# Rotary tables read back on GpSimd's queue, pooling-weight products in a fresh pair of tiles, value weights behind the query rows

## The chip, the cores and the metric

The kernel runs on one core of one Trainium2 chip. The metric is the device time of one execution in microseconds. The kernel before took 2415.74 us (median of 3 runs, 2414.28 to 2416.57).

A core has five engines with a queue each, worked off in order: PE (TensorE, matrix products into PSUM), ACT (ScalarE), DVE (VectorE), POOL (GpSimd) and SP (SyncE). An instruction that waits for a semaphore holds up everything behind it on its engine. Transfers are issued from the queues of SP, ACT and POOL; the instruction that issues one waits in its queue like any other, until the data to be sent are there and the place to be filled is free.

## The reference

One layer of a decoder trunk in float32, for 2048 tokens of width 1024 and 256 memory tokens:

```python
h = rmsnorm(x, mix_norm_g)
q, k, v, g, u = split(h @ w_in)                   # 4 heads of 128; u: 4 groups of 128 channels
y_ret  = silu(g) * head_rmsnorm(retention(rope(q), rope(k), v))
y_pool = pool_mixer(u, pool_w, pool_scale)        # trailing means, then a 128x128 product per group
x = x + concat(y_ret, y_pool) @ w_out
x = x + cross_attn(rmsnorm(x), rmsnorm(mem), wq, wkv, wo)
x = x + conv_glu_ffn(rmsnorm(x), w_up, conv, w_down)
return rmsnorm(x, final_norm_g)
```

`rope` turns each pair of halves of a head by an angle `position * inv_freq`: `t1 cos - t2 sin`, `t2 cos + t1 sin`.

## The kernel before

**Precision.** Every large product is made of three passes of TensorE: an operand is split into a rounded part (ACT, line 259 or 262) and a remainder (DVE, line 243 or 251), and high x high, high x low and low x high are added in PSUM (lines 271 to 273). So each weight tile costs, before it can be used, a load, two activations of 512 columns and two vector operations.

**Tiles and places.** SBUF is handed out in slots. `raws` are five places of 4 KB per partition for loaded weights, used in turn; `prs` are places for split pairs, to which free slots of the arenas G and E are lent; `Z` has eight slots of 4 KB per partition, `TT` (shown as T) ten of half that. A slot that is taken again waits for whatever still reads or writes it, a transfer from it included. `take()` hands out the slot that has been free for longest.

**Folded weights.** Two products of weights are made once, so that later stages need fewer: `folded_weights` is a generator of 32 steps that the program runs in portions, `folded(n)`. Steps 1 to 16 project the memory to keys and values (the values go to DRAM, `Vd`). Steps 17 to 20 (one per head) multiply the keys with the query weights: two loads of rows of `wqT` by `row_pairs` (line 497), 48 products of 256 columns, and the result to DRAM (`Md`, lines 548 and 501). Step 21 loads the pooling weights and three rows of `wout_p`; steps 22 to 24 multiply the four pooling groups `g` with their rows of the output projection (evacuation L592) and send each to DRAM (`WPd`, L594), and load `Vd` (L606). Steps 25 to 32 multiply the memory's values with `wo` (evacuation L633, stores to `VWd` L634).

In the loop over `g`, groups 0 and 1 take a Z slot each, and groups 2 and 3 write into the same two slots again.

**Opening.** Steps 1 to 20 run while tokens are loaded (`xR` for the norm, `xT` for the operand X), one step per turn `n` of a loop. In turns 16 to 19 the program calls `value_weights(n - 16)` (two rows of `w_v` into a raw place, split into a slot of G for the first two and of E for the others) and then `folded(1)`, which is one head of the query weights. After the loop come `values` (192 products), and beside them in `between()` the sums of quarters of X (`quarter_sums`) and, from the third call on, one step of `rope_steps(0)` per call.

**Rotary tables.** `rope_steps` loads the positions (two small transfers), computes sine and cosine on DVE in 11 steps in six T slots, and stores three tiles (sine, cosine, minus sine) to `rope_d`, on SP's queue (L2005). `scaled_tables`, a step generator inside the head projections, takes two Z slots, reads them back in four transfers on SP's queue (L1611), goes on with four steps of other splits, and then multiplies both tables with the norm's factors (four vector operations). They are used first where the second of eight pairs of projections is finished (`final`, kind < 2). Each of 56 items of the head projections (12 products of 512 columns) calls `step()` twice.

**Head projections to output projection.** The last items of the heads call steps 21, 22 and 23; after them come `folded(2)`, one more step for each step that is left of the last head's retention, and the output projection's eight `unit`s. Unit n loads four blocks of `wout_r` (L2118) and four of `WPd` (L2119) into one raw place and makes 48 products; block 4, the first one of `WPd`, is the fourth of the order. After units 0, 1 and 2 come 1, 2 and 4 more calls of `folded`.

**Sums of weights.** `weight_sums` adds blocks of the MLP's weights in DRAM by accumulating transfers from POOL's queue. It moves on by one round for every `spacing[0]` calls of `next(under[0])`, which `units` makes twice per unit if `paced[0]` is set. Before, it begins in the attention after the output projection of the first 1024 tokens.

**Order.** The order of instructions on each engine is set by a planner that runs over the program with its own estimate of times: earlier program order goes first where several are ready. `keep_in_program_order` and `issue_after` fix single places.

## Time and profile before

| | |
|---|---|
| runs, us | 2414.28, 2416.57, 2415.74 |
| profiled execution, us | 2421.08 |
| its span, us | 2419.3 |
| PE busy, us | 2390.1 (99%) |
| DVE, ACT, POOL busy, us | 1734.0 (72%), 1350.3 (56%), 276.0 (11%) |
| mean granted clock of TensorE | 0.997 |
| moved by DMA, MB | 511.53 |

A busy time is the union of an engine's instructions. A matmul of 512 columns is recorded as 0.38 us and starts 0.23 us after the one before it, so a PE that never waits shows 20.00 us of 20 and some 90 matmuls of that size. The chain of work that ended last is on PE for 94% of the span. The time that PE does not work is 29.2 us in all, and the views by windows tell in which stretches it lies.

### The profile page before, as it was taken

What the parts mean: (1) busy time and instruction counts of PE and PEld (TensorE: products, weight loads), DVE (VectorE), ACT (ScalarE), POOL (GpSimd) and SP (SyncE); (2) the same over time, 40 slices, a digit from 0 to 9 for tenths busy, and PEclk for the clock granted to TensorE, in tenths of its full rate; (3) what the DMA queues carried; (4) which work ended last, traced back from release to release, by engine and by line L of the source; (5) the groups of instructions that cost most, each with busy time, mean ns of one, the idle gap of its engine ahead of it and who ended that gap; (6) DMA issues with size and microseconds to landing.
All of it is one profiled execution on the core that took longest, in us unless ns stands there. A gap on an engine that the chain in (4) does not pass through costs nothing.

```text
span 2419.3 us, 33286 instructions
## 1 busy us (share of the span) xinstructions
PE 2390.1 (99%) x11186; PEld 1993.0 (82%) x11186; DVE 1734.0 (72%) x2904; ACT 1350.3 (56%) x2488; POOL 276.0 (11%) x437
## 2 busy tenths in 40 slices
PE   9999999999999999999999999999999999999998
PEld 8888878888888888888888888888888888887886
DVE  7787774754667665665789776987677698877876
ACT  7654564443445543434555555755555577676673
POOL 0010000063034444100001000110000000000000
PEclk9999999999999999999999999999999999999999
DMA  9732187499688799785477554765455479757952
GB/s 360 262 122 90 63 269 231 135 255 329 194 231 218 188 244 322 195 283 191 140 243 258 184 190 131 251 194 183 158 175 185 134 257 314 238 178 265 345 180 74
DMA packets 267451, 511.53 MB, mean 211 GB/s; under 512 B 29184, under 2 KB 58384, under 8 KB 267280
## 3 DMA queue, kind: packets, MB, share of 16 engines
q1 hardware_dynamic: 209312, 402.30, 50.1%
q0 software_dynamic: 32768, 77.61, 13.1%
q10 hardware_dynamic: 25200, 29.49, 3.5%
q8 instruction: 88, 1.44, 0.2%
q14 instruction: 83, 0.68, 0.1%
HBM read 397.61 MB, written 180.89 MB: 239 GB/s over the span
## 4 chain that ended last, share of the span: by engine, by line
PE 94%; DMA 2%; ACT 2%; DVE 1%; issue 0%; SPq 0%; ACTq 0%; DVEq 0%
PE mm L271 29%; PE mm L272 29%; PE mm L273 29%; PE aux L271 1%; PE aux L273 1%; PE aux L272 1%; ACT G L259 1%; PE aux L901 1%; DMA WPd<-Z 1%; PE aux L778 1%; DVE Z L243 1%; PE aux L806 1%; PE aux L790 0%; PE aux L808 0%; DMA R<-wkv 0%
## 5 line engine op out<-in xcount | busy, mean ns | idle before, releaser
L271 PE MATMUL mm<-G,Q 128*128 128x512 f32 (+1 forms) x1631 | 624.7, 384 | 6.9 <-ACT Q L259 2.7
L273 PE MATMUL mm<-G,Q 128*128 128x512 f32 (+1 forms) x1631 | 619.8, 383 | 0.8 <-DVE Q L243 0.8
L272 PE MATMUL mm<-G,Q 128*128 128x512 f32 (+1 forms) x1503 | 574.1, 382 | 0.2 <-DVE G L251 0.2
L272 PE MATMUL mm<-G,E 128*128 128x512 f32 (+1 forms) x1092 | 420.7, 385 | 0.0
L271 PE MATMUL mm<-G,E 128*128 128x512 f32 (+1 forms) x1092 | 419.2, 386 | 0.5 <-ACT E L259 0.5
L273 PE MATMUL mm<-G,E 128*128 128x512 f32 (+1 forms) x1092 | 418.4, 385 | 0.4 <-DVE E L243 0.4
L271 PEld LDWEIGHTS mm<-G,Q 128*128 128x128 f32 x1631 | 307.0, 188 | 69.2 <-ACT Q L259 4.0
L273 PEld LDWEIGHTS mm<-G,Q 128*128 128x128 f32 x1631 | 306.8, 188 | 60.6 <-DVE Q L243 1.8
L272 PEld LDWEIGHTS mm<-G,Q 128*128 128x128 f32 x1503 | 283.0, 188 | 53.5 <-DVE G L251 0.4
L243 DVE TENSOR_TENSOR Z<-Z,mm 128x512 f32<-128x512 f32 (+1 forms) x322 | 216.4, 676 | 124.6 <-PE mm L273 121.8
L251 DVE SCALAR_TENSOR_TENSOR Z<-Z,vecs 128x1024 f32<-128x1024 f32 x176 | 224.9, 1282 | 50.3 <-ACT Z L1134 48.0
L271 PEld LDWEIGHTS mm<-G,E 128*128 128x128 f32 x1092 | 205.3, 188 | 41.8 <-ACT E L259 0.7
L273 PEld LDWEIGHTS mm<-G,E 128*128 128x128 f32 x1092 | 205.3, 188 | 41.8 <-DVE E L243 0.7
L272 PEld LDWEIGHTS mm<-G,E 128*128 128x128 f32 x1092 | 205.3, 188 | 41.0
L1071 ACT ACTIVATE E<-R 128x512 fp32r<-128x512 f32 (+1 forms) x165 | 101.6, 616 | 146.9 <-PE mm L272 138.7
L243 DVE TENSOR_TENSOR Q<-R,Q 128x512 fp32r<-128x512 f32 x174 | 119.0, 688 | 53.0 <-ACT Q L259 34.7
L243 DVE TENSOR_TENSOR T<-T 128x512 f32<-128x512 f32 (+4 forms) x189 | 130.0, 692 | 23.4 <-ACT T L432 12.0
L243 DVE TENSOR_TENSOR G<-T,G 128x512 fp32r<-128x512 f32 (+1 forms) x173 | 113.8, 678 | 32.4 <-ACT G L1018 18.9
L1018 ACT ACTIVATE G<-T 128x512 fp32r<-128x512 f32 x186 | 111.8, 623 | 36.5 <-DMA T<-Gd 28.6
L1134 ACT ACTIVATE Z<-Z,vecs 128x1024 f32<-128x1024 f32 x88 | 109.2, 1242 | 31.8 <-DVE Z L243 30.8
L1071 ACT ACTIVATE E<-S 128x512 fp32r<-128x512 f32 (+1 forms) x107 | 65.9, 616 | 108.8 <-PE mm L272 106.9
L243 DVE TENSOR_TENSOR E<-R,E 128x512 fp32r<-128x512 f32 (+1 forms) x133 | 89.3, 675 | 43.8 <-ACT E L1071 43.1
(348 smaller groups left out, 3948.3 us busy)
## 6 DMA issues: line engine op xcount, KB each, us to landing
T<-Gd SPq DMA_DIRECT2D x173, 256.0 KB, 4.3
Ud<-w_up POOLq DMA_DIRECT2D x132, 256.0 KB, 9.1
Gd<-Z SPq DMA_DIRECT2D x110, 256.0 KB, 2.6
R<-Ud SPq DMA_DIRECT2D x106, 256.0 KB, 2.8
R<-w_up SPq DMA_DIRECT2D x80, 256.0 KB, 3.1
S<-Ud SPq DMA_DIRECT2D x70, 256.0 KB, 2.9
Gd<-T SPq DMA_DIRECT2D x56, 256.0 KB, 3.3
S<-w_up SPq DMA_DIRECT2D x52, 256.0 KB, 3.1
```

What stands on the lines that cost most here:

```text
L243: return eng.tensor_tensor(out=out, in0=a, in1=b, op=op)
L251: return dve.scalar_tensor_tensor(out=out, in0=a, scalar=s, in1=b, op0=op0, op1=op1)
L259: one = act.activation(hi, src, AF.Copy)
L271: pe.matmul(ps, lh, rh, start=start, stop=False, skip_group_check=more)
L272: pe.matmul(ps, lh, rl, start=False, stop=False, skip_group_check=more)
L273: latest[0] = pe.matmul(ps, ll, rh, start=False, stop=stop, skip_group_check=more)
L778: pe.matmul(col(sc, c), self.ch(k, c), self.ch(q, c), start=True, stop=True)
L806: pe.matmul(col(y, c), col(self.pr.f, c), self.ch(v, c, h * T), start=True, stop=self.cur[c] is None)
L901: pe.transpose(tp[:, j * P : (j + 1) * P], e.f[:, j * P : (j + 1) * P], ident)
L1018: one = act.activation(hi, x, AF.Copy, scale=-1.0 if i == 2 else 1.0)
L1071: act.activation(p2[:, 0, :w], self.raw[i].f[:, :w], AF.Copy)
L1134: act.activation(self.c[g].f, a[:, 2:], AF.Identity, bias=cb[:, f : f + 1], scale=cw[2][:, f : f + 1])
```

## The change

Five edits, all before or within the first half of the tokens:

1. Pooling groups 0 and 1 take, write and free a Z slot each; groups 2 and 3 share a fresh pair of neighbouring slots and go to DRAM in one transfer of 1 MB (three transfers for four).
2. The two halves (`mt`) of a step of the `wo` products are laid side by side and stored in one transfer instead of two.
3. The rotary tables of the first 1024 tokens: `rope_steps(0)` is begun, with five steps, at the end of the opening loop, and goes on by a step at every call of `between()`; its three stores are issued on ACT's queue, its four reads on POOL's; four empty steps are put ahead of the scaling.
4. `value_weights(0)` comes behind the second head's step of the query weights, 1 behind the third, 2 and 3 behind the fourth; the step goes first in each turn.
5. Calls of `folded` around the output projection: 2 instead of 1 per step of the last retention, then 2, 2, 2 after the units instead of 1, 2, 4. `paced` is set after the third unit, with a spacing of 3, instead of after the eighth.

```diff
-        vp4, held = G[:, 8 * T : 12 * T].rearrange("p (n i m) -> p n i m", i=2, m=NMEM), []
-        ended = []
+        vp4, ended = G[:, 8 * T : 12 * T].rearrange("p (n i m) -> p n i m", i=2, m=NMEM), []
         for g in range(4):
             u = ahead.pop(0)
-            if g < 2:
-                held.append(Z.take())
-            t = held[g % 2]
+            if g < 3:
+                held = Z.take(1 + g // 2)
+                t = held.f.rearrange("p (n k c) -> p n k c", n=KT, c=P)
...
-                done = act.activation(t.f[:, nh * SUB : (nh + 1) * SUB], ps, AF.Copy)
+                done = act.activation(t[:, 4 * nh : 4 * nh + 4, g % (held.n)], ps.rearrange("p (n c) -> p n c", c=P), AF.Copy)
             ended.append(done)
-            act.dma_start(WPd[:, :, g, :].rearrange("n p c -> p n c"), t.f.rearrange("p (n c) -> p n c", n=KT))
-            if g > 1:
-                t.free()
+            if g != 2:
+                act.dma_start(WPd[:, :, g + 1 - held.n : g + 1, :].rearrange("n p k c -> p n k c"), t)
+                held.free()
...
-                out = t.f[:, mt * SUB : (mt + 1) * SUB]
-                ended.append(act.activation(out, ps, AF.Identity, scale=rn[:, mt : mt + 1]))
-                act.dma_start(tiles4(VWd, nh, 2 * h + mt), out.rearrange("p (n c) -> p n c", n=4))
+                out = t.f.rearrange("p (n k c) -> p n k c", n=4, c=P)
+                ended.append(act.activation(out[:, :, mt], ps.rearrange("p (n c) -> p n c", c=P), AF.Identity, scale=rn[:, mt : mt + 1]))
+            act.dma_start(VWd[4 * nh : 4 * nh + 4, :, 2 * h : 2 * h + 2, :].rearrange("n p k c -> p n k c"), out)
...
-                sp.dma_start(out.f[p, i * T : (i + 1) * T].rearrange("p (s c) -> p s c", s=NS), rope_d[b][to].rearrange("(s p) c -> p s c", s=NS))
+                (sp if b else pool).dma_start(out.f[p, i * T : (i + 1) * T].rearrange("p (s c) -> p s c", s=NS), rope_d[b][to].rearrange("(s p) c -> p s c", s=NS))
...
             z.free(2, 2)
+            for _ in range(0 if b else 4):
+                yield
...
-            sp.dma_start(rope_d[b][i], r.f[:, :SUB])
+            (sp if b else act).dma_start(rope_d[b][i], r.f[:, :SUB])
...
+    tables = rope_steps(0)
     for n in range(1, 2 * KT + HEADS):
...
-        if 2 * KT <= n < 2 * KT + 4:
-            wv.append(value_weights(n - 2 * KT, B.arenas[(n - 2 * KT) // 2]))
         folded(1)
+        for kp in {2 * KT + 1: (0,), 2 * KT + 2: (1,), 2 * KT + 3: (2, 3)}.get(n, ()):
+            wv.append(value_weights(kp, B.arenas[kp // 2]))
+    for _ in range(5):
+        next(tables)
     reclaim(spare)
...
-        tables = iter(()) if b else rope_steps(0)
+        tables = iter(()) if b else tables
...
-            if place[0] > 2:
-                next(tables, None)
+            next(tables, None)
...
             for _ in behind[0]:
-                folded(1)
+                folded(2)
...
-                folded((1, 2, 4, 0, 0, 0, 0, 0)[n])
-        paced[0] = True
+                folded((2, 2, 2, 0, 0, 0, 0, 0)[n])
+                if n == 2:
+                    paced[0], spacing[0] = True, 3
```

## The prediction

> **What bounds the kernel now.** I read the busy table first (PE 99%), then busy time by windows, to see where the missing 29.2 us lie:

> ```profile
> core 0: us, PE busy (x) PEld busy (x) DVE busy (x) ACT busy (x) POOL busy (x), PEclk, DMA share, GB/s
> 0.00:80.00 80.00, 71.08 (x551) 68.53 (x552) 60.17 (x124) 66.03 (x125) 0.20 (x4) 1.00 0.95 352
> 80.00:280.00 200.00, 198.96 (x1011) 168.69 (x1011) 158.77 (x306) 99.67 (x209) 17.78 (x32) 1.00 0.38 127
> 280.00:360.00 80.00, 73.87 (x349) 58.81 (x348) 62.98 (x129) 55.14 (x124) 0.00 (x0) 0.98 0.61 203
> 360.00:780.00 420.00, 420.00 (x1947) 349.01 (x1946) 248.67 (x482) 186.74 (x382) 111.76 (x173) 1.00 0.79 229
> ```

> The change can win only where PE waits: 8.9 us in the opening, 1.0 in the head projections, 6.1 around the output projection. From 360 to 780 nothing is to be had. So this is a matter of at most some 16 us of 2416, and each edit is costed by the wait that it touches.

> **Value weights behind query rows.** In the opening, PE waits twice for ACT while the query weights are multiplied (waits of PE from 60 to 90, then ACT's timeline from 62 to 76):

> ```profile
> PE mm L271 <- ACT G L259: 3.4, 2, 2.2
> ...
> 62.82 0.63 ACT L259 ACTIVATE G<-S 128x512 fp32r<-128x512 f32 x1
> 63.34 0.63 ACT L259 ACTIVATE G<-S 128x512 fp32r<-128x512 f32 x1
> 66.00 0.67 ACT L259 ACTIVATE G<-R 128x512 fp32r<-128x512 f32 x1
> 67.04 0.68 ACT L259 ACTIVATE E<-R 128x512 fp32r<-128x512 f32 x1
> 68.61 0.66 ACT L259 ACTIVATE E<-R 128x512 fp32r<-128x512 f32 x1
> 69.12 0.66 ACT L259 ACTIVATE G<-R 128x512 fp32r<-128x512 f32 x1
> ...
> 60.00:80.00 20.00, 16.57 (x133) 15.96 (x132) 14.34 (x21) 18.86 (x41) 0.00 (x0) 1.00 0.95 322
> ```

> PE resumes on the activations at 66.00 and 69.12, splits of query rows. Ahead of the first stand two splits of value weights (62.82 and 63.34), ahead of the second two more (E, 67.04 and 68.61; E only ever holds value weights 2 and 3 here). ACT is busy for 18.86 of these 20 us, so it is the bound, and what leaves its queue ahead of a query row is won: four splits at a pitch of 0.52 us (63.34 less 62.82) are 2.1 us of the 3.4. Row loads also come sooner, since value weights no longer take a raw place ahead of them, so the wait can go whole. Bounds 0 (ACT's work is the same, and stays the limit) and -3.4; I take **-2.3**, near the counted splits. What the splits wait for afterwards: `values` needs weights 2 and 3 only after 24 products, 5.3 us into it (90 products take 20 us in the row of 100 to 120 below). The next 200 us of PE are dense (198.96 of 200), so time won here isn't lost behind it unless the tables are late.

> **Rotary tables.** Waits of DVE and of SP from 100 to 150, then of PE from 140 to 312:

> ```profile
> DVE Z L243 <- DMA Z<-rope: 4.4, 2, 3.1
> ...
> SPq L2005 <- ACT T L724: 10.2, 1, 10.2
> ...
> PE mm L271 <- DVE T L243: 0.3, 1, 0.3
> ```

> DVE stood 4.4 us for the tables, and SP 10.2 us for the sine with loads behind it; of all this 0.3 us reached PE, when a sum on DVE came late (0.4 with the restart). The tables' five first steps go 10 us and more earlier, to where DVE is not full:

> ```profile
> 80.00:100.00 20.00, 20.00 (x114) 17.60 (x114) 12.37 (x21) 11.65 (x25) 0.00 (x0) 1.00 0.98 340
> 100.00:120.00 20.00, 20.00 (x90) 16.57 (x89) 19.93 (x36) 7.92 (x13) 2.38 (x4) 1.00 0.36 129
> ...
> Z<-rope SPq DMA_DIRECT2D x4, 256.0 KB, 3.8
> Ad<-R POOLq DMA_DIRECT2D x22, 256.0 KB, 2.7
> ...
> Ud<-w_up POOLq DMA_DIRECT2D x132, 256.0 KB, 9.1
> ```

> The reads on POOL cost the price of its stores of the same size in the same stretch (100 to 300), 2.7 us to landing, and queue behind at most a few of those; SP is free for the projections' loads. The three stores on ACT are issues beside 7.92 busy us of 20. Four empty steps are two items of 12 products, 5.3 us; the first use comes three items (8.0 us) after the new place. I take **-0.4**; bounds -0.4 and 0: if the reads land as late as the slowest kind on POOL's queue (9.1 us, `Ud`), they are 5.3 us later than on SP (3.8), which the empty steps just cover.

> [...]

> **Pooling weights.** The waits of PE, then of ACT, from 320 to 350, the chain of that stretch, and two rows of ACT's timeline:

> ```profile
> PE mm L271 <- ACT Q L259: 2.0, 2, 1.3
> PE mm L271 <- ACT Z L592: 0.6, 1, 0.6
> PE mm L271 <- ACT Z L633: 0.6, 1, 0.6
> PE mm L271 <- DVE T L243: 0.5, 1, 0.5
> ...
> ACT Q L259 <- DMA R<-WPd: 4.2, 1, 4.2
> ACT G L259 <- DMA S<-Vd: 2.9, 1, 2.9
> ...
> 327.90 7.24 DMA WPd<-Z
> 336.28 5.61 DMA WPd<-Z
> 341.98 5.39 DMA R<-WPd
> ...
> 330.33 1.10 ACT L592 ACTIVATE Z<-mm 128x512 f32<-128x512 f32 x2
> 335.16 0.60 ACT L592 ACTIVATE Z<-mm 128x512 f32<-128x512 f32 x1 [1.59 <-DMA WPd<-Z]
> ```

> This is the change's main place. Group 3 is evacuated at 335.16 because its Z slot is still being stored (group 1's transfer, 7.24 us). ACT stands 1.6 us, and with it the evacuations and splits behind it; PE waits 1.3 us for a split (Q L259) and 0.6 for L633. Only then can group 3 be stored (5.61 us) and read back for unit 0 (5.39), which holds ACT 4.2 us and PE 0.7 more, the second wait for Q L259. With a fresh pair, group 3 follows group 2, which ACT evacuated at 330.33, so its store can go out by 332, over 4 us sooner, and one more `wo` step (12 products, 2.7 us) stands ahead of unit 0. That removes the waits of 2.0 and 0.6 us. PE was also slowed after these waits:

> ```profile
> 340.74 0.78 PE L273 MATMUL mm<-G,Q 128*128 128x512 f32 x1
> 341.31 0.63 PE L271 MATMUL mm<-G,Q 128*128 128x512 f32 x1
> 341.74 0.56 PE L272 MATMUL mm<-G,Q 128*128 128x512 f32 x1
> 342.13 0.39 PE L273 MATMUL mm<-G,Q 128*128 128x512 f32 x1
> ...
> 320.00:340.00 20.00, 16.98 (x75) 12.41 (x75) 16.63 (x41) 15.18 (x42) 0.00 (x0) 0.97 0.86 275
> 340.00:360.00 20.00, 19.31 (x83) 15.25 (x82) 12.17 (x19) 11.12 (x22) 0.00 (x0) 0.95 1.02 356
> ```

> Starts 0.57, 0.43 and 0.39 us apart, where 0.23 is usual, under a granted clock of 0.97 and 0.95: 0.03 and 0.05 of 20 us are 1.6 us of clock, of which I count 1.5. In all 2.0 + 0.6 + 1.5 = 4.1. The waits for L592 and DVE (1.1 us) come from `Vd` (2.9 us of ACT), which stays. The bounds: -5.2 with those too; and on the bad side one megabyte where half a one went. Two half ones took 7.24 and 5.61; if the one takes both, 12.9 us, it lands at 344.9, is read by 350.3, later than 347.37 by 2.9, against the 2.7 us of the extra step: nothing is won at unit 0, but the 1.3 and 0.6 us of the held ACT are. I take **-3.6**, half a microsecond short of the count, since DVE with 16.63 and ACT with 15.18 of 20 us will be nearer to full once the waits are out.

> [...]

> **The rest at nothing.** Side-by-side stores of the `wo` products halve issues on ACT, whose pace there is set by transfers. Sums of weights begin in units 3 to 7, in the stretch from 360 to 780 (first view), where PE is busy for 420.00 of 420 us, with and without POOL's sums beside it (111.76 us). Ten calls at a spacing of 3 are four rounds; the attention then makes two fewer of its own, so that the sums are two rounds ahead of before. The cover is the load ahead: if it went, a unit would wait for a load about once. I take 0, bounds 0 and +1.

> **The sum.** -2.3 - 0.4 - 3.6 = -6.3 us. The profiled execution took 2421.08 us for a span of 2419.3, so 1.8 us lie around the span and stay; it would take 2414.8. It is 5.3 us above the median of the runs, which is not of one place, so the same -6.3 us goes on the median: **2409.4 us**.

> **Rivals.**

> A. *The opening is not paid.* ACT's order changes, but its 18.86 of 20 us stay the limit, and other work (the split of X between the two, the evacuations) stands where the value weights stood. For it: the total work is the same. Against: half of it is needed only 5.3 us later. Time: -0.4 - 3.6, 2411.7.

> B. *The pooling wait moves.* The one megabyte lands as late as both halves, and ACT is held by `Vd` and the read as before. For it: a DMA share of 0.86 and 1.02 in these windows. Against: the store starts over 4 us earlier. Time: -2.3 - 0.4, 2413.0.

> C. *Slower: the positions block the opening.* The tables begin at the end of the opening, so their first T slots are those whose `Md` store is still under way, the positions' load waits for it on SP, and DVE, in order, waits for the positions. From 60 to 92:

> ```profile
> Md<-T ACTq DMA_DIRECT2D x16, 256.0 KB, 6.3
> T<-pos SPq DMA_DIRECT2D x2, 128.0 KB, 4.1
> ```

> That is 10.4 us from a store to the first table operation. If the planner, reckoning with shorter transfers, puts it on DVE ahead of the last head's low parts, PE has half a head left (24 products of 256 columns at 0.125 us, 133 in 16.57 busy us from 60 to 80, make 3.0): a stall of 7.4 us, with 1.5 of slow clock 8.9, and the opening isn't won: 8.9 - 0.4 - 3.6 = +4.9, 2420.6. It decides once the stall with its clock is over the 4.0 us that the other terms win. Against it: earlier program order goes first, and the last head's rows are loaded ahead of the positions.

> [...]

> E. *It does nothing*: the planner's new order opens as many gaps as it closes, 2415.7.

> F. *More*: both stretches are emptied (-3.4, -0.4, -5.2), 2406.7.

> **How the numbers follow.** Chances: forecast 0.48 (its own range 2407.5 to 2410.9), F 0.10, A 0.15, B 0.12, C 0.08, D 0.04, E 0.03. What a measurement of this kernel can tell from no change is 0.2%, 4.8 us. Faster: forecast and F, 0.58. Within 0.2%: A, B, D, E, 0.34. Slower: C, 0.08. The range runs from 2404.0 (F, and the spread of 2.3 us between the three runs) to 2416.0 (E); C and D lie outside.

> **What would show it.** *Value weights:* PE's wait for `G L259` between 60 and 90 under 1.2 us instead of 3.4, splits into E behind those of the last query rows. *Tables:* DVE's 4.4 us on `Z<-rope` gone; reads on POOL's queue landing in 2.7 to 4 us. *Pooling:* no wait of L592 for `WPd<-Z`; PE's wait for `Q L259` under 0.7 us and a granted clock of 1.00 from 320 to 360; PE busy from 280 to 360 over 76 us of 80. *Sums:* POOL busy from about 395, and PE still 20.00 of 20. I am wrong if PE waits in a new place between 70 and 130 (C), or if unit 0 still stands for `R<-WPd` (B).

## The result, and the profile after

The changed kernel takes 2421.40 us (median of 15 runs, 2418.63 to 2422.56) against 2416.48 us of the kernel before (15 runs, 2413.62 to 2417.72): a ratio of 1.0020, 95% interval 1.0012 to 1.0027. It is 4.9 us slower; 2409.4 was forecast, and the range ended at 2416.0.

The profiled execution of the changed kernel took 2421.4 us for a span of 2419.5. First the busy time by windows of the changed kernel, in the stretches of the prediction (columns: stretch and its length, busy us and count on PE, weight loads, DVE, ACT, POOL, granted clock, DMA share, GB/s):

```profile
0.00:80.00 80.00, 75.38 (x577) 72.36 (x578) 58.41 (x121) 66.41 (x127) 0.20 (x4) 1.00 0.96 357
80.00:280.00 200.00, 196.40 (x989) 165.79 (x987) 161.18 (x308) 98.50 (x207) 19.98 (x36) 1.00 0.37 125
280.00:360.00 80.00, 72.01 (x338) 57.11 (x337) 60.58 (x126) 53.97 (x122) 0.00 (x0) 0.98 0.59 200
360.00:780.00 420.00, 419.72 (x1938) 348.23 (x1937) 247.84 (x481) 188.19 (x388) 144.07 (x227) 1.00 0.90 256
...
60.00:80.00 20.00, 19.95 (x159) 19.24 (x159) 12.89 (x19) 19.65 (x44) 0.00 (x0) 1.00 0.98 337
130.00:150.00 20.00, 17.17 (x75) 13.61 (x74) 14.43 (x27) 7.06 (x12) 2.88 (x6) 1.00 0.55 163
```

PE works 4.3 us more than before in the opening (75.38 against 71.08), and 19.95 of 20 us between 60 and 80 where it had 16.57. It gives this back twice: 2.6 us between 80 and 280 (196.40 against 198.96), nearly all of it between 130 and 150, and 1.9 between 280 and 360 (2.8 against the second profile of before, which is told of below). Then a little from 360 to 780, where nothing was missing before. The waits of PE from 130 to 150 and from 320 to 350, and of DVE from 100 to 150, say for what:

```profile
PE mm L273 <- DVE Q L243: 1.5, 1, 1.5
PE mm L271 <- DVE T L243: 1.3, 1, 1.3
...
PE mm L271 <- ACT Z L632: 1.6, 1, 1.6
PE mm L271 <- ACT Z L591: 1.5, 1, 1.5
PE mm L271 <- DVE T L243: 1.4, 1, 1.4
PE mm L272 <- DVE G L243: 1.3, 1, 1.3
...
DVE R L243 <- DMA S<-w_qkgu: 3.3, 1, 3.3
```

DVE no longer stands 4.4 us for the tables; it stands 3.3 us for two blocks of the heads' weights instead, and PE behind it for 1.5 and 1.3 us. Lines 591 and 632 of this kernel are 592 and 633 of the one before: pooling groups and `wo` products. The issues of DMA of the changed kernel from 126 to 132 us (count, KB each, median us to landing):

```profile
Z<-rope POOLq DMA_DIRECT2D x4, 256.0 KB, 4.9
S<-w_qkgu SPq DMA_DIRECT2D x2, 256.0 KB, 6.3
```

And its chain of waits from 320 to 350 (start, duration, what):

```profile
321.22 7.01 DMA WPd<-Z
...
328.25 1.09 ACT Z L591 x2
...
335.88 7.43 DMA WPd<-Z
...
343.39 3.86 DMA R<-WPd
...
347.27 0.63 ACT G L259
347.90 0.58 ACT Z L632
```

Group 1 (328.25) waits for the store of group 0, and the joint store of one megabyte goes out at 335.88 and lands at 343.31: 1.4 us later than the last half did before (336.28 and 5.61 us). Unit 0's read holds ACT until 347.27, and PE stands 1.6 us at 347 for the evacuation behind it (L632).

A second profile of the kernel before was taken with the experiments (2417.45 us, near its median), since the first, at 2421.08, was above every one of its 15 runs. For each time of before, I counted the matrix columns that PE has started by then; the table shows how much later the changed kernel has started as many (a minus sign: earlier). "Ahead" and "behind" mean this count from here on:

| at us of before | 80 | 160 | 300 | 400 | 1000 | 2100 | 2300 |
|---|---|---|---|---|---|---|---|
| against the first profile | -3.8 | -0.3 | -0.2 | +2.6 | +3.5 | +4.0 | -0.3 |
| against the second | -5.8 | -3.2 | -3.3 | +1.7 | +2.6 | +3.4 | +3.4 |

The last column of the first row holds a loss of 4.3 us near 2205 us in that one execution, two gaps and a clock of 0.50 behind them, from 2209.16 to 2212.57 (27.84 of 30 us of PE between 2190 and 2220; 30.00 in the second profile and in the changed kernel; tables_alone, below, has one such gap of 1.1 us at 2205). So the prediction's own base was a bad execution: it laid the 5.3 us above the median on no place, and 4.3 of them were there.

### The profile page after: what moved, and what is told of

It reads as the page before. It is cut to its first block, busy times and chain, and to the rows that moved or that the text cites. A ratio compares the mean times of both kernels' runs of the same rounds, so it can differ in the third digit from the quotient of the medians.

```text
span 2419.5 us, 33291 instructions
## 1 busy us (share of the span) xinstructions
PE 2391.3 (99%) x11186; PEld 1993.3 (82%) x11186; DVE 1734.2 (72%) x2904; ACT 1350.2 (56%) x2488; POOL 277.8 (11%) x441
## 4 chain that ended last, share of the span: by engine, by line
PE 94%; DMA 2%; ACT 2%; DVE 1%; issue 0%; SPq 0%; POOL 0%; ACTq 0%; DVEq 0%
PE mm L271 29%; PE mm L273 29%; PE mm L272 29%; PE aux L271 1%; PE aux L272 1%; PE aux L273 1%; DMA WPd<-Z 1%; ACT G L259 1%; PE aux L900 1%; DVE Z L243 1%; PE aux L777 1%; PE aux L805 1%; PE aux L789 0%; PE aux L807 0%; PE aux L363 0%
## 5 line engine op out<-in xcount | busy, mean ns | idle before, releaser
L271 PE MATMUL mm<-G,Q 128*128 128x512 f32 (+1 forms) x1617 | 619.6, 384 | 4.1 <-DVE T L243 1.3
L273 PE MATMUL mm<-G,Q 128*128 128x512 f32 (+1 forms) x1617 | 614.2, 383 | 2.1 <-DVE Q L243 2.1
L272 PE MATMUL mm<-G,Q 128*128 128x512 f32 (+1 forms) x1489 | 568.8, 382 | 0.3 <-DVE G L251 0.2
L272 PE MATMUL mm<-G,E 128*128 128x512 f32 (+1 forms) x1092 | 420.5, 385 | 0.0
L273 PE MATMUL mm<-G,E 128*128 128x512 f32 (+1 forms) x1092 | 418.3, 385 | 1.1 <-DVE E L243 1.1
L271 PE MATMUL mm<-G,E 128*128 128x512 f32 (+1 forms) x1092 | 419.0, 386 | 0.2 <-ACT G L1017 0.2
L271 PEld LDWEIGHTS mm<-G,Q 128*128 128x128 f32 x1617 | 304.5, 188 | 65.4 <-ACT Q L259 1.7
L273 PEld LDWEIGHTS mm<-G,Q 128*128 128x128 f32 x1617 | 304.2, 188 | 61.4 <-DVE Q L243 3.1
L272 PEld LDWEIGHTS mm<-G,Q 128*128 128x128 f32 x1489 | 280.6, 188 | 53.4 <-DVE G L251 0.7
L243 DVE TENSOR_TENSOR Z<-Z,mm 128x512 f32<-128x512 f32 (+1 forms) x322 | 215.2, 672 | 124.1 <-PE mm L273 122.2
L273 PEld LDWEIGHTS mm<-G,E 128*128 128x128 f32 x1092 | 205.2, 188 | 42.4 <-DVE E L243 1.3
L272 PEld LDWEIGHTS mm<-G,E 128*128 128x128 f32 x1092 | 205.2, 188 | 41.4 <-DVE G L243 0.4
L271 PEld LDWEIGHTS mm<-G,E 128*128 128x128 f32 x1092 | 205.1, 188 | 41.3 <-ACT G L1017 0.6
L243 DVE TENSOR_TENSOR Q<-R,Q 128x512 fp32r<-128x512 f32 x176 | 119.8, 686 | 53.4 <-ACT Q L259 37.0
L243 DVE TENSOR_TENSOR T<-T 128x512 f32<-128x512 f32 (+4 forms) x196 | 134.2, 689 | 22.7 <-ACT T L432 12.4
L243 DVE TENSOR_TENSOR G<-T,G 128x512 fp32r<-128x512 f32 (+1 forms) x169 | 110.2, 673 | 29.4 <-ACT G L1017 16.7
L243 DVE TENSOR_TENSOR E<-R,E 128x512 fp32r<-128x512 f32 (+1 forms) x135 | 90.2, 672 | 43.6 <-ACT E L1070 42.6
## 6 DMA issues: line engine op xcount, KB each, us to landing
T<-Gd SPq DMA_DIRECT2D x168, 256.0 KB, 4.5
Ud<-w_up POOLq DMA_DIRECT2D x132, 256.0 KB, 10.0
Gd<-Z SPq DMA_DIRECT2D x110, 256.0 KB, 2.9
R<-Ud SPq DMA_DIRECT2D x106, 256.0 KB, 2.8
R<-w_up SPq DMA_DIRECT2D x80, 256.0 KB, 3.0
S<-Ud SPq DMA_DIRECT2D x70, 256.0 KB, 2.9
Gd<-T SPq DMA_DIRECT2D x56, 256.0 KB, 3.4
T<-Xd SPq DMA_DIRECT2D x53, 256.0 KB, 4.3
```

Of the source, the lines that this page charges most:

```text
L243: return eng.tensor_tensor(out=out, in0=a, in1=b, op=op)
L271: pe.matmul(ps, lh, rh, start=start, stop=False, skip_group_check=more)
L272: pe.matmul(ps, lh, rl, start=False, stop=False, skip_group_check=more)
L273: latest[0] = pe.matmul(ps, ll, rh, start=False, stop=stop, skip_group_check=more)
```

## The experiments

Theory at the start, from the two traces: *terms add up*. Edit 3 costs 2.8 us at 137 to 149 us, edit 1 some 3 us at 300 to 400, edit 5 0.9 at 899, and edit 4 wins 3.8. The main rival, *slack*: what is won in the opening is lost at the next limit whatever edit 3 does. All results in one table (medians of 11 runs, 5 for paced_late; beside each the kernel before, run along with it):

| kernel | us | before | ratio | 95% interval |
|---|---|---|---|---|
| opening_alone (edit 4) | 2420.50 | 2416.67 | 1.0019 | 1.0010 to 1.0027 |
| tables_alone (edit 3) | 2417.61 | 2416.67 | 1.0006 | 0.9997 to 1.0014 |
| pooling_alone (edit 1) | 2417.06 | 2416.67 | 1.0000 | 0.9991 to 1.0009 |
| sums_alone (edits 2, 5) | 2419.75 | 2416.67 | 1.0009 | 1.0000 to 1.0018 |
| tables_back (all but 3) | 2421.83 | 2416.92 | 1.0020 | 1.0011 to 1.0029 |
| angles_out | 2416.04 | 2416.92 | 0.9995 | 0.9986 to 1.0004 |
| own_slots | 2422.71 | 2416.92 | 1.0025 | 1.0016 to 1.0033 |
| four_slots_alone | 2416.87 | 2416.92 | 1.0001 | 0.9992 to 1.0009 |
| no_sums (all but 5) | 2419.58 | 2417.42 | 1.0009 | 1.0001 to 1.0018 |
| opening_and_tables (3, 4) | 2417.34 | 2417.42 | 0.9999 | 0.9990 to 1.0008 |
| scaled_on_pool | 2419.54 | 2417.42 | 1.0010 | 1.0001 to 1.0019 |
| reads_late | 2415.91 | 2416.32 | 1.0000 | 0.9991 to 1.0009 |
| reads_on_sp | 2414.69 | 2416.32 | 0.9996 | 0.9987 to 1.0005 |
| paced_late | 2425.93 | 2416.32 | 1.0041 | 1.0029 to 1.0054 |
| sp_and_four_slots | 2416.09 | 2416.45 | 0.9999 | 0.9990 to 1.0008 |

*Terms add up* does not hold: the four kernels with the edits alone add up to a ratio of 1.0034, or +8.2 us, where the change has 1.0020. Edits 3 and 4 are the clearest case: 1.0006 and 1.0019 alone, 0.9999 together.

### The edits one by one

Each kernel is the one before with the lines of the change's diff that belong to its edits and no others.

opening_alone:

```diff
-        if 2 * KT <= n < 2 * KT + 4:
-            wv.append(value_weights(n - 2 * KT, B.arenas[(n - 2 * KT) // 2]))
         folded(1)
+        for kp in {2 * KT + 1: (0,), 2 * KT + 2: (1,), 2 * KT + 3: (2, 3)}.get(n, ()):
+            wv.append(value_weights(kp, B.arenas[kp // 2]))
```

> The kernel before with edit 4 alone (value weights behind query rows). In the changed kernel PE was 3.8 us ahead of before at 80 us (same work done) and had lost that again by 380 us. Theory 'terms add up': the opening's gain is its own and nothing behind it needs it back, so PE is 3 to 4 us ahead at 80 us and still at the end: 2412.5 to 2413.5 against 2416.5. Rival 'slack': the weights' and tables' loads of the head projections set the pace behind the opening, whatever the opening does; then the gain is gone by 150 us, with new waits of PE between 120 and 150, and the time is 2416.5 plus or minus 0.7.

2420.50: the opening is won (4.1 us at 80 us against the first profile), and it is the edit that costs most. Waits of DVE from 100 to 150 and of PE from 130 to 150 of this kernel:

```profile
DVE Z L243 <- DMA Z<-rope: 3.5, 1, 3.5
...
PE mm L273 <- DVE S L243: 1.5, 1, 1.5
PE mm L271 <- DVE T L243: 1.3, 1, 1.3
```

Its waits of PE from 245 to 305, then its busy time by windows:

```profile
PE aux L821 <- ACT T L816: 2.0, 1, 2.0
PE mm L271 <- ACT Q L1708: 1.2, 1, 1.2
...
130.00:150.00 20.00, 17.17 (x74) 13.56 (x74) 11.33 (x20) 9.70 (x15) 1.08 (x2) 1.00 0.51 154
...
300.00:320.00 20.00, 18.48 (x97) 15.54 (x98) 15.05 (x27) 12.87 (x25) 0.00 (x0) 0.91 0.29 86
```

Of the two, *slack* has the place: with the old tables the same 2.8 us are lost between 130 and 150, now since DVE stands 3.5 us for the tables. Its time, 2416.5, was missed all the same, since neither theory had the second loss, at the heads' end: PE waits 1.2 us at 251 and 2.0 at 297, and the granted clock falls behind it (0.91 from 300 to 320). The kernel before has no wait at the first of these places and 0.8 us at the second. The loss comes with a new order of the heads' instructions on PE. tables_back, below, has the same two waits, and no kernel with edits 3 and 4 together has them, so it belongs to edit 4 without edit 3; why the planner chose that order I haven't settled.

> The kernel before with edit 3 alone (rotary tables begun five steps early, stores on ACT's queue, reads on POOL's, four empty steps). Theory 'terms add up': the 2.8 us that the changed kernel lost between 137 and 149 us come from this edit by itself, 2419.3, with PE waiting there for sums and splits of DVE (L243). Rival 'collision': they come only since the heads begin 3 us sooner (edit 4 too); alone, the edit has the old slack, and the time is 2416.5 plus or minus 0.7.

The diff is edit 3 in the change's diff. Measured +0.9 us; the interval holds both theories. In its trace PE waits 1.6 us at 149.5 for a sum on DVE (T L243) where the first profile of before has 0.3, so part of the loss is the edit's own, and it comes without edit 4.

> The kernel before with edit 1 alone (groups 0 and 1 free their Z slot at once, groups 2 and 3 in a pair, one store of 1 MB). Theory 'the wait moved': group 1 gets group 0's slot again, its evacuation waits for group 0's store (3 to 7 us), and the 1 MB store lands no sooner than the two halves did; no gain at unit 0, 1 to 3 us lost ahead of it: 2417.5 to 2419.5. Rival 'the sums': what the changed kernel lost from 297 to 380 us (2.9 us) belongs to the doubled calls of folded there (edit 5), and edit 1 alone wins part of the 3.6 us that were forecast: 2413 to 2415.5.

The diff is edit 1. Measured +0.4, interval around no change. Its trace has group 1's evacuation waiting 1.0 us for the store of group 0, and the joint store goes out at 334.30 and takes 8.80 us. So the wait did move, though it costs nothing here that can be measured; the forecast gain isn't there either.

> The kernel before with edits 2 and 5 alone (stores of the wo products side by side; folded called 2 for 1 per step of the last retention, 2, 2, 2 behind the units; sums of weights from the third unit on with a spacing of 3). Theory 'the wait moved': this edit costs only the 0.9 us lost near 899 us, 2417.4, or nothing. Rival 'the sums': the 2.9 us from 297 to 380 are of the extra step of the folded weights ahead of unit 0, 2419.4.

The diff is edits 2 and 5. Measured +3.1 (ratio 1.0009, up to 1.0018): the forecast had 0, bounds 0 and +1. In its trace PE's waits at 379 us (0.3) and 900 us (0.6) are those of the changed kernel. It has another of 3.0 us at 337, behind a pooling store that took 8.4 us instead of 7.2. Whether that one is of the edit stays open: PE and ACT have the old order up to there, but SP sends the loads beside this store in another order from 330 us on.

### What takes the opening's gain

tables_back is the changed kernel with the lines of edit 3 undone. angles_out is the changed kernel without the steps on DVE that compute the angles; its tables are sines of the bare positions, so it doesn't compute the layer:

```diff
         b3 = pt.f[:, :SUB]
+        if not b:
+            for _ in range(10):
+                yield
+            act.activation(b2, b3, AF.Sin)
+            act.activation(sm, b3, AF.Sin, bias=half_pi, scale=-1.0)
+            for v in (pt, A, B1, N_):
+                v.free()
+            yield S_, B2
+            return
```

> The changed kernel without edit 3 (rotary tables begun, stored and read as before). Theory 'VectorE is the bound': then the tables come late instead of the weights, DVE stands for Z<-rope at 139 to 143 us as with edit 4 alone, and the opening's 3.8 us are lost in the same place all the same: 2421 to 2422.5. Rival 'edit 3 costs': the early steps and the reads on POOL lose it, and without them 2 us or more are kept: 2419.4 or less.

> The changed kernel with the computation of the rotary angles of the first 1024 tokens left out (the ten steps on DVE issue nothing; the tables are sines of the bare positions; loads, stores, reads and scaling stay). Theory 'VectorE is the bound behind the opening': its 13 us of angle operations stand between the loads and the first heads' sums; without them the gaps of PE at 137 and 147 us (3.1 us) are gone and PE is at 160 us still 2.5 us or more ahead of before (0.3 in the changed kernel): 2418 to 2419. Rival 'queues': the gap at 137 comes from weights' loads beside the four reads on POOL's queue (6.3 us to landing, otherwise 2.7); it stays, and the time is 2420.5 to 2421.4.

tables_back is as slow as the change (2421.83): with edit 3 or without it, the gain is lost. angles_out is 5.4 us faster than the changed kernel, and its gaps at 137 and 147 are gone. The busy time of angles_out from 130 to 150:

```profile
130.00:150.00 20.00, 20.00 (x90) 16.57 (x89) 14.91 (x27) 8.73 (x14) 1.10 (x2) 1.00 0.28 93
```

The loads of these weights among the DMA issues, of angles_out from 112 to 132 us, and of the first profile of before from 110 to 132:

```profile
S<-w_qkgu SPq DMA_DIRECT2D x2, 256.0 KB, 3.7
```

```profile
S<-w_qkgu SPq DMA_DIRECT2D x2, 256.0 KB, 2.8
```

Not all of the 5.4 us are won at this place. angles_out is 3.1 us ahead of the first profile of before at 160 and 1.6 at 400; the changed kernel is 0.3 ahead and 2.6 behind. So the angle operations are worth some 2.8 us here, the rest lies behind 300 us, and beside the kernel before even angles_out shows no gain (0.9995, interval around no change).

How the loads come to be late begins with the first sum of quarters of X on DVE, of the first profile of before, of the changed kernel and of angles_out (start, busy, what, idle before):

```profile
88.29 0.69 DVE L243 TENSOR_TENSOR S<-S 128x512 f32<-128x512 f32 x1 [6.95 <-ACT T L1564]
```

```profile
95.38 0.69 DVE L243 TENSOR_TENSOR S<-S 128x512 f32<-128x512 f32 x1 [3.23 <-ACT T L1563]
```

```profile
96.15 0.69 DVE L243 TENSOR_TENSOR S<-S 128x512 f32<-128x512 f32 x1 [12.02 <-ACT T L1573]
```

The sums begin 7.1 us later than before, and not for DVE's early angle steps (begun at 84.9 us): DVE is idle ahead of them, longest where there are no angle steps. It waits for ACT's copy of a quarter (L1563, 94.64 instead of 87.54). That copy is late in every kernel with edit 3 (93.1 to 95.4 us, against 84.3 to 89.0 in all others); in the changed kernel it stands behind two evacuations of `values`, and why the planner puts it there isn't settled. From the first sum to the first of the two loads it is then 34.4 us, against 26.8 before. That is not for more angle steps, of which 8.0 us stand in this stretch and 9.3 before: eight remainders of the sums (`G<-Z,G`), which before came behind the weights' splits that free the raw places, now stand ahead of them, and DVE is idle for 2.4 us. In angles_out, without the angle steps and with the remainders behind again, it is 21.2 us. The loads go out at 129.80 and 130.41 instead of 115.08 and 119.58 (117.36 and 120.92 in angles_out), together, beside four reads of the tables, and land after 6.3 us instead of 2.8.

So angles_out takes out two things at once, DVE's work and the meeting of loads and reads. The next kernels are to tell one from the other. opening_and_tables is the kernel before with edits 3 and 4; the others differ from it by one thing each:

```diff
--- reads_on_sp
-                (sp if b else pool).dma_start(out.f[p, i * T : ...
+                sp.dma_start(out.f[p, i * T : ...
--- reads_late
+            for _ in range(0 if b else 4):
+                yield
             for to, half in ((0, 0), (0, 1), (2, 0), (1, 1)):
...
             z.free(2, 2)
-            for _ in range(0 if b else 4):
-                yield
--- scaled_on_pool
-                    tt(dve, d, d, rb[s].f[:, :SUB], ALU.mult)
+                    tt(dve if b else pool, d, d, rb[s].f[:, :SUB], ALU.mult)
```

> The kernel before with edits 3 and 4 alone, the two that make one whole. Theory 'VectorE is the bound': 3.8 us are won by 80 us, 3.5 lost again by 160 as in the changed kernel, and nothing changes behind: 2416 to 2417 against 2416.5. Rival 'loss': as with edit 4 alone, the heads' end is worse placed and 2 us or more are lost between 280 and 360: 2418.5 or more.

> As opening_and_tables, with the four reads of the tables on SP's queue as before. Theory 'collision': whatever the queue, the reads and the weights' loads share the same microseconds; the loads still take 5 us or more, the gap at 137 stays over 1.5 us, 2417.3 plus or minus 0.7. Rival 'GpSimd's queue': it is the second queue that slows SP's loads; in SP's order they land in under 4 us, and 1.5 us or more are won.

> As opening_and_tables, with the four empty steps ahead of the four reads of the tables instead of behind them, so that the reads go out behind the two weights' loads of 129.5 and 130.2 us, which took 7.5 us to landing beside the reads. Theory 'collision': alone, these loads land in 3 to 4.5 us, the gap of PE at 137 (2.8 us) is under 1 us, and the kernel is 1.5 to 2.5 us faster than opening_and_tables (2417.3): 2415 to 2416. Rival 'VectorE is the bound': DVE then stands for the tables instead (Z<-rope, as with edit 4 alone), the gap moves to 140 to 150 us, and the time stays 2417.3 plus or minus 0.7.

> As opening_and_tables, with the four multiplications that scale the tables of the first 1024 tokens (2.8 us of DVE) moved to POOL, so that DVE neither makes them nor stands for Z<-rope. Theory 'VectorE is the bound': the gaps of PE at 137 and 147 us (3.1 us) shrink to 1.5 or less, and the kernel is 1.5 to 3 us faster than opening_and_tables: 2413.5 to 2415.5. Rival 'late tables': POOL takes so much longer over them that the first heads wait for the tables, the gap at 147 grows, and it is no faster than opening_and_tables.

Issues of DMA from 126 to 132, first of opening_and_tables, then of reads_on_sp:

```profile
Z<-rope POOLq DMA_DIRECT2D x4, 256.0 KB, 5.8
S<-w_qkgu SPq DMA_DIRECT2D x2, 256.0 KB, 7.6
```

```profile
Z<-rope SPq DMA_DIRECT2D x4, 256.0 KB, 4.8
S<-w_qkgu SPq DMA_DIRECT2D x2, 256.0 KB, 5.2
```

Edits 3 and 4 together are worth nothing (2417.34 against 2417.42): 4.1 us ahead of the first profile of before at 80 us, 1.4 behind at 160, 0.7 ahead at 400. With the reads on SP's queue the loads take 5.2 us instead of 7.6 and PE's wait at 137 falls from 2.7 to 0.5 us, but 1.5 and 0.5 us appear behind it, at 147 and 144, for sums on DVE. Other traces bear this out: in the five kernels that are alike up to here with the reads on POOL's queue (the changed kernel, no_sums, own_slots, paced_late, opening_and_tables) the loads take 6.3 to 7.6 us and PE's first wait is 1.5 to 2.7 us; in the two with the reads on SP's (reads_on_sp, sp_and_four_slots) 5.2 and 5.6, and 0.5 and 0.8. All of PE's gaps from 135 to 152 together are 2.3 to 4.2 us in the five and 2.5 and 2.3 in the two. So both were true in part: with the reads on POOL's queue the gap at 137 was larger, and where it was smaller, waits for DVE came behind it. The time, 2414.69, is the lowest of the study; its interval still holds no change, and by the ratios it is 0.7 us from opening_and_tables, well within the intervals.

reads_late missed its aim: the planner issued the reads at 126.28 as before. What moved was the four splits that stand between reads and scaling; as I read the program, they come after the first products that use them, so those products take operands from before the splits. The kernel computes other heads than the reference, and its time says nothing on the question.

scaled_on_pool lost 2.2 us where 1.5 to 3 were to be won, by a way that no theory had: PE's wait at 138 grew from 2.7 to 5.3 us, and the granted clock fell behind it (0.83 from 130 to 150). DVE's timeline from 137.5 and POOL's (start, busy, what, idle before):

```profile
138.78 0.69 DVE L243 TENSOR_TENSOR S<-R,S 128x512 f32<-128x512 f32 x1
139.40 3.33 DVE L243 TENSOR_TENSOR R<-R 128x512 f32<-128x512 f32 x1
142.65 1.28 DVE L243 TENSOR_TENSOR Q<-R,Q 128x512 fp32r<-128x512 f32 x2
...
139.67 2.49 POOL L243 TENSOR_TENSOR Z<-Z,T 128x512 f32<-128x512 f32 x2
```

An operation of 0.69 us on DVE took 3.33 while POOL made two multiplications beside it: 2.49 + 0.69 = 3.2.

### Pooling slots

own_slots is the changed kernel in which group 0's slot is freed after group 1 has taken its own; four_slots_alone is the kernel before with four slots and four stores:

```diff
--- own_slots
-                held.free()
+                if g:
+                    held.free()
+                    first = first and first.free()
+                else:
+                    first = held
--- four_slots_alone
-            if g < 2:
-                held.append(Z.take())
-            t = held[g % 2]
+            held.append(Z.take())
+            t = held[-1]
...
-            if g > 1:
-                t.free()
+            for r in (held if g == 1 else [t] if g else []):
+                r.free()
```

> The changed kernel, but group 0 keeps its Z slot until group 1 has taken its own. Theory 'slot order': the wait of group 1's evacuation for group 0's store (L591 for WPd<-Z, 1.7 us of PE at 327 us) is gone, and 1 to 2 us with it: 2419.4 to 2420.4 against 2421.4 of the changed kernel. Rival 'one megabyte': the joint store of groups 2 and 3 still goes out behind 334 us and takes 7 us or more, unit 0 still waits for it, and what PE doesn't wait at 327 it waits between 338 and 349: 2421.4 plus or minus 0.5.

> The kernel before, but each of the four pooling groups has a Z slot of its own and its own store of half a megabyte. Theory 'slot order and one megabyte': neither of the two waits is left, group 3's store goes out 2 to 4 us sooner than at 336.28, lands sooner than 341.89, and 1 to 3 us are won: 2413.5 to 2415.5 against 2416.5. Rival 'transfers': the stores share the DMA engines with the loads (DMA share near 1 there), so what starts sooner takes longer, the read for unit 0 lands near 347 as before: 2416.5 plus or minus 0.7.

own_slots took 2422.71, no less than the changed kernel. Waits of ACT and PE from 320 to 350, of own_slots:

```profile
ACT Z L591 <- DMA WPd<-Z: 3.6, 1, 3.6
...
PE mm L271 <- ACT G L259: 5.0, 1, 5.0
```

Slots are handed out by when the program freed them, and it frees a slot right behind the store's issue. In the changed kernel group 0 takes slot 1 when no other is free, and frees it at once; the next ones come free later in program order, so for group 1 slot 1 is the one that has been free for longest, and it gets it with the store under way. With group 0's slot held, group 1 gets slot 7, and the fresh pair for groups 2 and 3 is slots 6 and 7: now the pair waits for group 1's store, 3.6 us of ACT and 5.0 of PE. The wait goes wherever the slot goes. Neither theory had that.

With four slots no evacuation waits, the last half lands at 340.24 (343.81 in the second profile of before), and PE's wait for `R<-WPd` is gone: 75.91 of 80 us from 280 to 360, against 74.84 in that second profile. The time is the same even so (2416.87). Part of it goes again behind the stretch. The waits of PE and ACT from 360 to 380 of this kernel:

```profile
PE mm L271 <- ACT G L259: 1.3, 1, 1.3
...
ACT Z L632 <- DMA Z<-xR: 3.7, 1, 3.7
```

PE's 1.3 us, at 367.9, are for a split (G L259) that stands in ACT's queue, busy without a break since 364.8; the second profile of before has no wait of PE here. ACT's 3.7 us come later (372.5, a `wo` product gets a Z slot with a load in it), and PE doesn't wait for them. So without any wait in the pooling groups the stretch to 360 holds about 1 us to be won, not 3.6, and this kernel loses it again by 370.

### Sums of weights, and the sum

no_sums is the changed kernel without edit 5; paced_late is the changed kernel with

```diff
-                if n == 2:
-                    paced[0], spacing[0] = True, 3
+        paced[0] = True
```

> The changed kernel without edit 5 (calls of folded and sums of weights as before). Theory 'the sums cost': the gaps at 379 us (0.4) and 899 us (0.7), and one step of the folded weights fewer ahead of unit 0, are worth 1 to 2.5 us: 2419 to 2420.4 against 2421.4 of the changed kernel. Rival 'nothing': the steps left out ahead of unit 0 stand behind it, 2421.4 plus or minus 0.5.

> The changed kernel with the sums of weights begun as before (paced set behind the eighth unit, without the spacing of 3); the calls of folded stay 2, 2, 2. Theory 'sums early': the 0.9 us near 899 us are gone and 0.5 to 1 us of the 2 that edit 5 costs, 2420.4 to 2421. Rival 'folded': all of edit 5's cost is in the placing of the folded steps (the gap at 379 us and ahead of unit 0), nothing changes: 2421.4 plus or minus 0.4, and the gap at 899 stays.

> The kernel before once more, for a second profile of it. Its first profiled execution took 2421.08 us, 4.6 above the median of its runs. Theory 'one execution's stall': the 2.2 us that PE lacks between 2190 and 2220 and the clock halved around 2210 and 340 us belong to that execution; the second profile has the time between 2414 and 2418 and lacks at least the stall at 2205. Rival 'always there': both places look as in the first profile, and the time of the profile is 2420 or more.

> As reads_on_sp (edits 3 and 4 with the reads of the tables on SP's queue), with a Z slot and a store of its own for each of the four pooling groups. Theory 'gains add': 1.6 us of reads_on_sp and what the wait of group 3 costs, 0.5 to 1 us more: 2413.5 to 2415, below both kernels. Rival 'the transfers set the pace': the read for unit 0 lands no sooner, as with the four slots alone, and the time is that of reads_on_sp, 2414.7 plus or minus 0.7, or that of before.

Leaving edit 5 out wins 1.8 us against the changed kernel's 2421.40, or 2.7 by the two ratios to the kernel before. paced_late is the surprise: with the sums begun as late as before, but `folded` placed as changed, it takes 2425.93. Windows from 890 to 910, first paced_late, then no_sums:

```profile
890.00:910.00 20.00, 16.34 (x62) 12.93 (x61) 9.68 (x15) 6.47 (x13) 9.57 (x16) 0.83 1.07 336
```

```profile
890.00:910.00 20.00, 20.00 (x90) 16.55 (x89) 12.81 (x20) 8.95 (x18) 10.12 (x17) 1.00 1.07 322
```

The loss is at 898 us, where the second half of the tokens begins its output projection: PE waits 3.7 us, and the granted clock falls behind it (0.83 from 890 to 910, 1.00 in no_sums). Full DMA engines alone don't explain it, for their share is 1.07 in both kernels. By its chain paced_late waits there for the load `S<-WPd`, issued at 893.47; no_sums issues the same load at 893.16 and PE doesn't wait. With `folded` placed as changed the early sums don't cost; they pay back most of this loss (0.6 us of PE's wait are left in the changed kernel). How 2, 2, 2 instead of 1, 2, 4 steps near 360 us makes PE wait at 898 is not settled.

no_sums is 2.2 us slower than opening_and_tables: that is edits 1 and 2 behind edits 3 and 4, though edit 1 alone cost nothing. In no_sums the joint store took 9.03 us and PE stood 2.6 us for its read; its waits between 135 and 152 were also 0.9 us longer than those of opening_and_tables, from the same instructions. With intervals of 2 us either way this is an indication, not more.

before_again has no stall at 2205 and no halved clock near 340 us (1.00 from 280 to 360), but two windows at 0.50 in the opening (67.95 to 74.77); sp_and_four_slots (reads_on_sp with the four slots) took 2416.09, so the two don't add, and no version here is faster than before beyond its interval.

## Why the prediction was wrong

**Value weights.** The step was right, and better than forecast: -3.8 us by 80 us instead of -2.3, beyond its bound of -3.4, and the wait for `G L259` is gone. The step that failed is the sentence behind it: "The next 200 us of PE are dense (198.96 of 200), so time won here isn't lost behind it unless the tables are late." A dense PE only shows that the work behind came just in time at the old pace. The condition at the end of the sentence was the case: in opening_alone and tables_back DVE stands 3.5 us for the tables. In the changed kernel, 0.3 of the 3.8 us are left at 160.

**Rotary tables.** Forecast -0.4, bounds -0.4 and 0; in the changed kernel's trace it loses 2.8 us. The step "go 10 us and more earlier, to where DVE is not full" counted DVE's free time (12.37 of 20 us) but not what the move does to the order of the work: the sums of quarters begin 7.1 us later, behind ACT's copy, eight remainders come ahead of the weights' splits, and the two loads go out 14.7 and 10.8 us later. And I costed the reads by POOL's stores of the same stretch, 2.7 us: they took 4.9, and the loads beside them 6.3. That price was also misread. 2.7 us is the median of 22 stores from 100 to 300; the four that POOL sent while DVE was at 19.93 of 20 us, from 112 to 117, took 3.5 and 3.6.

With DVE at 5.38 of 6 us from 126 to 132 the reads on POOL's queue took 4.9 us in the changed kernel. Moved to SP's queue they took 4.8 instead of the 5.8 of opening_and_tables, so by these two kernels about 1 us at most is of the queue, an estimate. The loads beside them took 7.6 us with the reads on POOL's queue and 5.2 with them on SP's, against 2.8 in the first profile of before: on either queue they were late beside the reads.

**Pooling weights.** Forecast -3.6; alone it is 0, and there are signs of +2 behind the other edits. Two steps failed. "Group 3 follows group 2, which ACT evacuated at 330.33, so its store can go out by 332": ACT evacuated group 2 at 332.73 and group 3 at 334.72, and a joint store waits for the later one; it went out at 335.88. And "no wait of L592 for `WPd<-Z`" holds for groups 2 and 3 only: I took the pair's slots as fresh, but not what freeing group 0's slot at once does to group 1. The bad bound came true in its mechanism (one megabyte landed at 343.31, the last half of before at 341.89 and 343.81 in its two profiles), and its size was still too good, since it counted ACT's waits of 1.3 and 0.6 us as won. Rival B, which had the same mechanism and counted nothing as won, is what pooling_alone measured.

**The rest.** Forecast 0, bounds 0 and +1; measured +2.2 by its ratio, 0 to 4.3. The sums began at 384 us instead of 478, and their lead did not shrink as the forecast had it: by the count of POOL's transfers they were 41 ahead at 500, 48 at 780 and 42 at 900. And "a unit would wait for a load about once" was priced at 1 us at most; the units at 898 were not looked at, and what the placing of `folded` does to them was put at nothing.

**The slow clock.** I gave 1.5 us to it as a consequence of the waits at 335. The clock was halved there in the first profile of before (0.50 from 338.65 to 342.06) and not in the second (1.00 from 280 to 360). How much of this term the median of before holds is not known.

**Rivals and range.** C did not happen: PE waits nowhere between 70 and 130; that its 2420.6 is near the measured 2421.40 is chance. E, "opens as many gaps as it closes", fits edits 3 and 4 exactly and had 3 in 100. The two slower rivals, C and D, were left outside the range at 0.12 together, and each rival moved one term and left the others as won. The result is three terms lost at once. I take them to hang together, since each leans on the same slots, places and DMA engines; that edits 3 and 4 do is measured (the ratios alone and together), for the others it is not.

## What to carry to other kernels

A stretch in which the bound engine is 99% busy can have the next limit close behind it, as this one had. Before you count time won ahead of it as kept, look how much slack the loads and the vector engine have there, and what queues behind a step that you move forward, also for places and slots. Where slots are handed out by program order, freeing one earlier can give the next taker a slot whose transfer is still under way, as here, so write down who gets which. And profile the kernel before twice when a change is worth 0.2%.

## What the runs showed of the hardware

```profile
64.54:67.95 3.41, 1.26 (x10) 1.05 (x10) 1.49 (x3) 3.41 (x10) 0.00 (x0) 1.00 1.05 391
67.95:71.36 3.41, 2.60 (x13) 2.30 (x12) 3.23 (x5) 3.41 (x7) 0.00 (x0) 0.50 1.02 375
71.36:74.77 3.41, 3.41 (x18) 3.41 (x17) 2.65 (x5) 1.40 (x4) 0.00 (x0) 0.50 1.00 306
```

```profile
335.24:338.65 3.41, 1.91 (x7) 0.86 (x5) 3.41 (x9) 3.41 (x7) 0.00 (x0) 1.00 0.99 343
338.65:342.06 3.41, 3.05 (x10) 2.58 (x11) 3.20 (x6) 3.41 (x12) 0.00 (x0) 0.50 1.16 343
```

```profile
296.31:299.72 3.41, 2.01 (x12) 1.39 (x13) 2.11 (x4) 3.34 (x8) 0.00 (x0) 1.00 0.33 130
299.72:303.13 3.41, 3.41 (x9) 2.63 (x10) 2.72 (x5) 2.02 (x4) 0.00 (x0) 0.50 0.25 32
303.13:306.54 3.41, 3.40 (x21) 2.87 (x20) 2.77 (x5) 3.12 (x6) 0.00 (x0) 1.00 0.30 121
```

Neither PE's busy share of a window nor its longest gap tells by itself which window was followed by a halved one. In the changed kernel the window ahead of the halving is 0.59 busy, with gaps of 0.84 and 0.56 us and none longer, and PE starts 9 matmuls in the halved window and 21 in the one behind it; the window from 327.02 is 0.55 busy with a gap of 1.52 us and was followed by one at full speed (1.00). In the first profile of before, the windows from 2205.75 (0.46 busy) and 335.24 (0.56) were followed by a halved one, and the one from 65.58 (0.54) was not. And in the last 20 us a window of 0.89, from 2405.74 in the changed kernel, was followed by one at 0.50.

The same stall lay in one window in one execution and across two in another: the opening's stall halved the clock in the second profile of before, where the window from 64.54 is 0.37 busy, and not in the first, where the windows meet at 65.58, within the stall, and are 0.70 and 0.54 busy.

**An operation of VectorE took 3.33 us beside two of GpSimd.** This is the one at 139.40 in scaled_on_pool, above, seen once: the other two multiplications on POOL, at 132.08, fell into a time when DVE had nothing to do (6.38 us idle up to 138.06). One row of POOL's groups by line from 120 to 150 of scaled_on_pool (busy us, mean ns of one):

```profile
L243 POOL TENSOR_TENSOR Z<-Z,T 128x512 f32<-128x512 f32 x4 | 5.0, 1281 | 1.4 <-DMA Z<-rope 1.3
```

The multiplication took 1281 ns on POOL; on DVE the same four took 688 ns each in the first profile of before. That DVE stood for POOL's two is my estimate from the sum above (2.49 + 0.69 = 3.2 us); no other run shows it.
